# Elementwise work taken off GpSimd in a scheduled eight-core decoder trunk, with new planning costs and six square tiles

## The chip, the cores and the metric

The kernel runs on the 8 cores of one Trainium2 chip, one sequence of the batch per core, with no communication between the cores. The metric is the time of one execution in device microseconds (us) on the slowest core. An execution can fall into a slow state: the cores of one die (cores 0 to 3, or 4 to 7), or of both, are granted a lower TensorE clock than in the other executions, and the time is longer. I compare fast executions with fast ones, and I read core 4.

## The reference, cut to what matters

```python
D_MODEL = 1024; BATCH = 8; SEQ = 2048; DEPTH = 2; D_FF = 2816

def modulate(x, g, mod):                       # every sub-layer begins with this
    shift, scale, gate = jnp.split(mod, 3, axis=-1)
    h = rmsnorm(x, g) * (1.0 + scale[:, None, :]) + shift[:, None, :]
    return h, gate[:, None, :]

def swiglu(h, w_in, w_out):
    g, u = jnp.split(h @ w_in, 2, axis=-1)
    return (jax.nn.silu(g) * u) @ w_out

# layer 0: SwiGLU, gated mixer AB, SwiGLU;  layer 1: SwiGLU, pooling mixer, SwiGLU; final RMSNorm
mod = c_act @ w_mod[l] + b_mod[l]              # (B, 9*D), one row per output of the conditioning
x = x + 0.5 * gate * swiglu(h, w_ffn_in[l, 0], w_ffn_out[l, 0])
...
```

Everything is float32 in the reference. The kernel multiplies in float16.

## The kernel before

Each core keeps its whole residual stream `X` on chip and goes through ten *phases*: four SwiGLUs and one AB mixer, each for two halves of 1024 tokens (`p` = 0, 1). The pooling mixer runs in the background of other phases. The SwiGLU input projection is a Strassen-like product with 7 instead of 8 block products. It needs sums of blocks of the weights (`piece_sums`) and of `H` (`h_sums`). Between two phases, at a *boundary*, the last down-projection of one phase adds into `X` and squares it for the next RMSNorm, while the `H` of the next phase is built for the other half of the tokens.

The program is not written in its final order. A list scheduler places each instruction at the earliest gap of its engine by *planned* costs and latencies, and each engine is given its list in that order. Where two engines are offered ("flex"), the one planned to end first is taken.

```python
class Sched:
    LAT = {"pe": 0.27, "act": 0.10, "dve": 0.10, "pool": 0.12, "sp": 0.05}
    ...
        choices = eng if isinstance(eng, list) else [(eng, fn, cost)]
        for e, f, c in choices:
            ...                                   # ready = latest of the dependences' ends + LAT
            t = self.tl[e].find(ready, c)
            if best is None or t + c < best[0] - 1e-9:
                best = (t + c, t, e, f, c)
    ...
    def c_act(n, src="ps"):
        return (0.20 if src == "ps" else 0.40) + n / 1200.0
    def c_dve(n, half=False):
        return 0.20 + n / (1920.0 if half else 960.0)
    def c_pool(n):
        return 0.20 + n * 1.9e-3
    def tt_(out, in0, in1, op, reads, writes, n=TT, half=False, flex=False):
        f = I("tensor_tensor", out=out, in0=in0, in1=in1, op=op)
        if flex:
            return add([("dve", f, c_dve(n, half)), ("pool", f, c_pool(n))], None, reads=reads, writes=writes)
        return add("dve", f, reads=reads, writes=writes, cost=c_dve(n, half))

    def piece_sums(pc):                           # block sums of a weight piece, float16
        tt_(v(4), v(2), v(3), ALU.add, [k(2), k(3)], [k(4)], half=True, flex=True)
        ...                                       # three more
    def square(c, t):                             # on ScalarE or GpSimd
        q = sq_rot.next()                         # one of NSQ = 4 tiles
        op = add([("act", I("activation", ..., func=AF.Square), c_act(TT, "sb")),
                  ("pool", I("tensor_tensor", ..., op=ALU.mult), c_pool(TT))], ...)
    tmp_rot = Rot((6, 7))                         # two normalisation tiles
    def apply_chunk(l, s, p, c, tt, place):       # H = X * rstd * scale + shift
        tm = tmp_rot.next()
        tt_(TP[:, tm, 0:TT], Xv(c, t), RS[:, t, :], ALU.mult, ..., flex=True)
        act(place.ap(c, tt), TP[:, tm, 0:TT], AF.Identity, ..., scale=AS[...], bias=MODT[...])

    # class Down, at the end of each of its 16 units of the last down-projection:
                stt(Xv(dch, t), PS[bk][:], GH[...], Xv(dch, t), ALU.mult, ALU.add, ...)   # residual
                if self.last:
                    self.flush_ones(NSQ - 1)      # TensorE sums earlier squares over partitions
                    self.sq.append((square(dch, t), t))
    ...
    def run_down(dn, rest):
        for n, (_, f) in enumerate(rest[:-1]):
            f()
            pump()                                # background work, and every 7th time a row product
```

A *row product* multiplies one row of `w_mod` with the conditioning vector on VectorE (`WMOD<-WMOD,CB` in the profile, in two halves of 512). There are 144 rows, 16 of them before the first phase can start.

## Time and profile before

| | before |
|---|---|
| executions before the prediction | 2138.98, 2265.44, 2384.79 us; one more, profiled, 2215.79 us (slow) |
| core 4 of the profile: span | 2127.6 us |
| TensorE (PE), VectorE (DVE), ScalarE (ACT), GpSimd (POOL) busy on core 4 | 1985, 1446, 901, 677 us |

The list of cores (core: span, mean granted clock) shows which cores to read. The first die was disturbed.

```profile
core 4: 2127.6 us, clock 0.967
...
die 0 (median of its cores): 2185.6 us, clock 0.947
die 1 (median of its cores): 2129.1 us, clock 0.969
```

From the page of core 4, part 1 (busy us, share, number of instructions) and the first line of part 4 (the chain of waits followed back from the end):

```profile
PE 1985.1 (93%) x9440; PEld 913.4 (43%) x9440; DVE 1446.4 (68%) x2530; ACT 900.6 (42%) x1462; POOL 676.7 (32%) x707
...
PE 85%; DVE 12%; ACT 1%; DMA 1%; issue 0%; SPq 0%; DVEq 0%
```

TensorE bounds the kernel, but 12% of the chain passes through VectorE. Where that is, the stretches show. Each line is a window in us from the start; after its length come busy us and instructions of each engine, the granted clock (1.00 is the highest in the record), and the DMA share. The first five are boundaries, the sixth is the middle of a phase.

```profile
270.00:299.00 29.00, 16.70 (x72) 6.67 (x71) 28.83 (x34) 14.38 (x21) 21.97 (x16) 0.85 0.32 75
705.00:740.00 35.00, 25.60 (x116) 11.00 (x115) 33.11 (x35) 19.39 (x29) 31.02 (x24) 0.92 0.36 61
925.00:965.00 40.00, 30.35 (x136) 12.97 (x135) 38.90 (x51) 20.14 (x30) 31.82 (x26) 0.93 0.43 103
1150.00:1195.00 45.00, 33.36 (x148) 14.07 (x147) 43.36 (x58) 20.18 (x31) 33.89 (x27) 0.92 0.43 95
1375.00:1417.00 42.00, 36.54 (x163) 15.80 (x162) 34.98 (x46) 23.47 (x36) 24.98 (x21) 0.96 0.30 51
...
1450.00:1550.00 100.00, 100.00 (x519) 48.43 (x518) 55.97 (x91) 43.33 (x70) 27.12 (x29) 1.00 0.45 78
```

TensorE is not idle in this stretch in the middle of a phase, and at the boundaries it idles for 5 to 12 us while VectorE is occupied for 83 to 99% of the time. The clock also falls below 1.00 there: behind most of these gaps the clock record of this trace stands at 0.50 for 7 to 14 us, from the steady start (the first matmul of the steady stream, at 64.6 us) to the last matmul. Ten matmuls at half clock took 4.47 us, and ten at full clock (1.00) 2.32 us. At one boundary two gaps, 1.44 and 2.67 us with three matmuls between them, went before it: the record has 0.50 from 1413.4 us, 1.0 us into the second gap, and the ten matmuls from 1415.84 us on took 4.47 us.

Are those VectorE microseconds work? The groups of VectorE's instructions, by shape (count | busy us, mean ns of one | idle before), answer that:

```profile
L318 DVE TENSOR_TENSOR ACTB<-TP,ps 128x512 f16<-128x512 f32 x368 | 250.9, 686 | 113.0 <-PE ps L318 81.8 <-ACT ps L318 27.9
L318 DVE SCALAR_TENSOR_TENSOR X<-ps,GH,X 128x512 f32<-128x512 f32 x320 | 235.1, 747 | 197.6 <-PE ps L318 197.2
L318 DVE TENSOR_TENSOR SLOTS<-SLOTS 128x512 f16<-128x512 f16 x478 | 227.8, 496 | 11.6 <-POOL SLOTS L318 5.2 <-DMA SLOTS<-win 1.1
L318 DVE SCALAR_TENSOR_TENSOR WMOD<-WMOD,CB 128x512 f32<-128x512 f32 x256 | 216.5, 874 | 0.0
...
L318 DVE TENSOR_TENSOR TP<-X,RS 128x512 f32<-128x512 f32 x89 | 100.1, 1136 | 7.3 <-ACT H L318 4.0 <-ACT WMOD L318 3.3
L318 DVE TENSOR_TENSOR H<-H 128x1024 f16<-128x1024 f16 x64 | 62.2, 991 | 2.2 <-ACT H L318 1.5
```

`TP<-X,RS` (normalisation) and `ACTB<-TP,ps` both take two inputs of 512 elements, but the one with two inputs in SBUF takes 1136 ns and the one with an input in PSUM 686. (`ps`, the tiles that matmuls write to, lies in PSUM; the other tiles named here lie in SBUF.) A piece of the timeline at a boundary (start us, us, engine, instruction, idle before) shows what happens:

```profile
1401.85 1.99 DVE L318 TENSOR_TENSOR H<-H 128x1024 f16<-128x1024 f16 x1
...
1401.99 2.98 POOL L318 TENSOR_TENSOR TP<-X,RS 128x512 f32<-128x512 f32 x2
```

One H sum lasts 1.99 us when a GpSimd normalisation runs beside it. Of the 64 H sums in this trace 39 last 0.68 or 0.69 us; 32 of them overlap no two-input instruction of GpSimd, 7 do. The other 25, of 0.85 to 2.16 us, all overlap one, by 0.41 us or more. The residual additions, with one input in PSUM, average 745 ns where they overlap one and 748 where they do not. So I take part of VectorE's busy time for waiting. I call this lengthening of instructions with two SBUF inputs beside GpSimd's the *exclusion* of the two engines.

### The profile page before, as it was taken

What the parts mean: (1) busy time and instruction counts of PE and PEld (TensorE: products, weight loads), DVE (VectorE), ACT (ScalarE), POOL (GpSimd) and SP (SyncE); (2) the same over time, 40 slices, a digit from 0 to 9 for tenths busy, and PEclk for the clock granted to TensorE, in tenths of its full rate; (3) what the DMA queues carried; (4) which work ended last, traced back from release to release, by engine and by line L of the source; (5) the groups of instructions that cost most, each with busy time, mean ns of one, the idle gap of its engine ahead of it and who ended that gap; (6) DMA issues with size and microseconds to landing.
All of it is one profiled execution on the core that took longest, in us unless ns stands there. A gap on an engine that the chain in (4) does not pass through costs nothing.

```text
span 2214.1 us, 26222 instructions; the slowest of 8 cores (2125.3 to 2214.1 us)
## 1 busy us (share of the span) xinstructions
PE 2069.2 (93%) x9440; PEld 933.4 (42%) x9440; DVE 1444.3 (65%) x2530; ACT 900.9 (41%) x1462; POOL 676.9 (31%) x707
## 2 busy tenths in 40 slices
PE   2799979999999899989999799999999999999996
PEld 0344434444545344434444344444454345534442
DVE  6856887476767866686557863466565756575654
ACT  3433444045252551444214440355455544554242
POOL 5313353123111621162213431142244323442310
PEclk9999988889999999998889888899999999999998
DMA  9795948577666468756858474454635463536752
GB/s 278 149 234 111 174 91 145 109 132 149 114 113 125 76 102 164 125 116 114 147 110 147 92 114 65 64 81 67 95 57 77 59 104 53 81 51 101 145 86 76
DMA packets 71245, 248.75 MB, mean 112 GB/s; under 512 B 6992, under 2 KB 7120, under 8 KB 70608
## 3 DMA queue, kind: packets, MB, share of 16 engines
q0 software_dynamic: 46928, 153.63, 48.1%
q1 hardware_dynamic: 24192, 93.45, 13.4%
q8 instruction: 79, 1.29, 0.2%
q14 instruction: 46, 0.38, 0.1%
HBM read 392.28 MB, written 8.39 MB: 181 GB/s over the span
## 4 chain that ended last, share of the span: by engine, by line
PE 84%; DVE 12%; DMA 2%; ACT 1%; issue 0%; SPq 0%; DVEq 0%
PE ps L318 84%; DVE TP L318 2%; DVE X L318 2%; DVE SLOTS L318 2%; DVE WMOD L318 2%; DMA WMOD<-wmod 2%; DVE H L318 2%; DVE ACTB L318 1%; DVE MODT L318 0%; ACT H L318 0%; ACT SQ L318 0%; ACT RS L318 0%; DVE ps L318 0%; ACT ps L318 0%; SPq L318 0%
## 5 line engine op out<-in xcount | busy, mean ns | idle before, releaser
L318 PE MATMUL ps<-H,SLOTS 128*128 128x512 f16 x5440 | 1271.7, 394 | 88.8 <-DVE H L318 27.1
L318 PEld LDWEIGHTS ps<-H,SLOTS 128*128 128x128 f16 x5440 | 544.3, 101 | 774.3 <-issue 299.2
L318 PE MATMUL ps<-ACTB,SLOTS 128*128 128x512 f16 x3072 | 734.5, 395 | 0.0
L318 ACT ACTIVATE ps<-ps 128x512 f32<-128x512 f32 x528 | 307.3, 582 | 702.7 <-PE ps L318 670.1
L318 PEld LDWEIGHTS ps<-ACTB,SLOTS 128*128 128x128 f16 x3072 | 310.2, 101 | 388.0 <-issue 108.7
L318 DVE SCALAR_TENSOR_TENSOR X<-ps,GH,X 128x512 f32<-128x512 f32 x320 | 235.1, 746 | 221.6 <-PE ps L318 221.2
L318 DVE TENSOR_TENSOR ACTB<-TP,ps 128x512 f16<-128x512 f32 x368 | 251.5, 687 | 142.1 <-PE ps L318 103.0
L318 POOL TENSOR_TENSOR SLOTS<-SLOTS 128x512 f16<-128x512 f16 x226 | 286.8, 1272 | 182.8 <-DVE SLOTS L318 166.5
L318 POOL DMA_DIRECT2D SLOTS<-win x176 | 99.5, 565 | 781.0 <-PE ps L318 749.8
L318 ACT ACTIVATE TP<-ps 128x512 f32<-128x512 f32 x400 | 238.8, 597 | 202.1 <-PE ps L318 202.0
L318 DVE TENSOR_TENSOR TP<-ps,TP 128x512 f32<-128x512 f32 x176 | 121.5, 691 | 268.8 <-ACT ps L318 268.1
L318 DVE SCALAR_TENSOR_TENSOR WMOD<-WMOD,CB 128x512 f32<-128x512 f32 (+1 forms) x262 | 225.5, 888 | 16.5 <-DMA WMOD<-wmod 16.5
L318 DVE TENSOR_TENSOR SLOTS<-SLOTS 128x512 f16<-128x512 f16 x478 | 227.4, 495 | 11.7 <-POOL SLOTS L318 5.1
L318 ACT ACTIVATE SQ<-X 128x512 bf16<-128x512 f32 x165 | 103.2, 630 | 254.3 <-DVE X L318 200.8
L318 POOL TENSOR_TENSOR TP<-X,RS 128x512 f32<-128x512 f32 x103 | 148.0, 1443 | 64.5 <-ACT H L318 58.5
L318 DVE TENSOR_TENSOR ps<-ps,TP 128x512 f32<-128x512 f32 x176 | 122.9, 698 | 45.9 <-PE ps L318 45.7
L318 ACT ACTIVATE H<-TP,MODT,AS 128x512 f16<-128x512 f32 x160 | 125.8, 803 | 49.2 <-DVE TP L318 24.7
L318 POOL DMA_DIRECT2D SLOTS<-wout x64 | 47.1, 735 | 239.5 <-PE ps L318 232.4
L318 PE MATMUL ps<-SQ,ONES 128*128 128x512 bf16 x232 | 86.0, 407 | 29.9 <-ACT SQ L318 25.4
L318 DVE TENSOR_TENSOR TP<-X,RS 128x512 f32<-128x512 f32 x89 | 98.0, 1113 | 7.1 <-ACT H L318 4.0
L318 POOL TENSOR_TENSOR SQ<-X 128x512 bf16<-128x512 f32 x59 | 63.0, 1080 | 38.4 <-DVE X L318 18.2
L318 DVE TENSOR_TENSOR H<-H 128x1024 f16<-128x1024 f16 x64 | 62.2, 990 | 2.2 <-ACT H L318 1.5
(68 smaller groups left out, 515.1 us busy)
## 6 DMA issues: line engine op xcount, KB each, us to landing
SLOTS<-win POOLq DMA_DIRECT2D x176, 512.0 KB, 6.0
WMOD<-wmod SPq DMA_DIRECT2D x134, 512.0 KB, 6.2
SLOTS<-wout POOLq DMA_DIRECT2D x32, 768.0 KB, 9.5
SLOTS<-wout POOLq DMA_DIRECT2D x32, 640.0 KB, 8.2
SLOTS<-wab POOLq DMA_DIRECT2D x28, 512.0 KB, 7.4
X<-xT SPq DMA_DIRECT2D x4, 2048.0 KB, 17.4
outT<-X SPq DMA_DIRECT2D x16, 512.0 KB, 5.3
ACTB<-wmod SPq DMA_DIRECT2D x10, 512.0 KB, 21.1
```

The costliest lines, as they stand in the source:

```text
L318: return lambda E: getattr(E, name)(*a, **k)
```

## The change

Its intent is to leave GpSimd with loads and a few tiny instructions, to plan with costs nearer to the measured ones, and to relieve VectorE at the boundaries. The core of the diff:

```diff
-    LAT = {"pe": 0.27, "act": 0.10, "dve": 0.10, "pool": 0.12, "sp": 0.05}
+    LAT = {"pe": 0.27, "act": 0.16, "dve": 0.14, "pool": 0.12, "sp": 0.05}
-    NSQ = 4
+    NSQ = 6
-        return (0.20 if src == "ps" else 0.40) + n / 1200.0
+        return (0.10 if src == "ps" else 0.18) + n / 1200.0
-        return 0.20 + n / (1920.0 if half else 960.0)
+        return 0.09 + n / (1920.0 if half else 960.0)
...    # tt_ loses flex: block sums and normalisations always on VectorE
-        op = add([("act", I("activation", out=SQ[:, q, :], in_=Xv(c, t), func=AF.Square), c_act(TT, "sb")),
-                  ("pool", I("tensor_tensor", out=SQ[:, q, :], in0=Xv(c, t), in1=Xv(c, t), op=ALU.mult), c_pool(TT))],
-                 None, reads=[Xk(c, t)], writes=[("SQ", q)])
+        op = act(SQ[:, q, :], Xv(c, t), AF.Square, [Xk(c, t)], [("SQ", q)], src="sb")
...    # pump(rows=...) : row products are left out where rows is False
     def run_down(dn, rest):
         for n, (_, f) in enumerate(rest[:-1]):
             f()
-            pump()
+            pump(rows=not dn.last)
...    # pm_consts (bands of the pooling mixer): uses RS instead of TP tiles, called after the first loads
```

More of the change, by code (lines that the diff above doesn't have):

```diff
@@ L391, in act, with tt_ @@
         return add("act", I("activation", out=out, in_=in_, func=func, **kw), reads=reads, writes=writes, cost=c_act(n, src))
-    def tt_(out, in0, in1, op, reads, writes, n=TT, half=False, flex=False):
-        f = I("tensor_tensor", out=out, in0=in0, in1=in1, op=op)
-        if flex:
-            return add([("dve", f, c_dve(n, half)), ("pool", f, c_pool(n))], None, reads=reads, writes=writes)
-        return add("dve", f, reads=reads, writes=writes, cost=c_dve(n, half))
+    def tt_(out, in0, in1, op, reads, writes, n=TT, half=False):
+        return add("dve", I("tensor_tensor", out=out, in0=in0, in1=in1, op=op), reads=reads, writes=writes, cost=c_dve(n, half))
     def stt(out, in0, scalar, in1, op0, op1, reads, writes, n=TT, **kw):
@@ L514, in k @@
             return ("SL", s, q)
-        tt_(v(4), v(2), v(3), ALU.add, [k(2), k(3)], [k(4)], half=True, flex=True)
-        tt_(v(2), v(0), v(2), ALU.subtract, [k(0), k(2)], [k(2)], half=True, flex=True)
-        tt_(v(5), v(4), v(0), ALU.subtract, [k(4), k(0)], [k(5)], half=True, flex=True)
-        tt_(v(6), v(1), v(5), ALU.subtract, [k(1), k(5)], [k(6)], half=True, flex=True)
+        tt_(v(4), v(2), v(3), ALU.add, [k(2), k(3)], [k(4)], half=True)
+        tt_(v(2), v(0), v(2), ALU.subtract, [k(0), k(2)], [k(2)], half=True)
+        tt_(v(5), v(4), v(0), ALU.subtract, [k(4), k(0)], [k(5)], half=True)
+        tt_(v(6), v(1), v(5), ALU.subtract, [k(1), k(5)], [k(6)], half=True)
     wm_rot = Rot(range(NWM))
@@ L633, in bg_step, with pump @@
             bg_state[0] = 0.0
-    def pump(n=1):
+    def pump(n=1, rows=True):
         for _ in range(n):
@@ L638, in pump @@
                 bg_step()
-        rows_pump()
+        if rows:
+            rows_pump()
     def bg_drain():
@@ L728, in apply_chunk @@
         tm = tmp_rot.next()
-        tt_(TP[:, tm, 0:TT], Xv(c, t), RS[:, t, :], ALU.mult, [Xk(c, t), ("RS", t)], [("TP", tm)], flex=True)
+        tt_(TP[:, tm, 0:TT], Xv(c, t), RS[:, t, :], ALU.mult, [Xk(c, t), ("RS", t)], [("TP", tm)])
         act(place.ap(c, tt), TP[:, tm, 0:TT], AF.Identity, [("TP", tm)] + fin["k", l, s, c], [place.key(c, tt)], src="sb",
@@ L944, in ab_phase @@
             ab_consts()
-        bsb = [SQ, None]
-        def proj(lhs_slot, col, c, tt, b, first, last, cols=slice(0, TT), rhs=None):
-            pass
         def v_stats(tt, n):
@@ L1070, in pm_consts @@
             add("dve", I("memset", INVC[:, k:k + 1], 1.0 / (k + 1)), writes=[("INVC", k)], cost=0.1)
-        onesf = TP[:, 0, 0:128]
-        eye = TP[:, 1, 0:128]
-        rot = Rot(range(2, 8))
-        add("dve", I("memset", onesf, 1.0), writes=[("TP", 0)], cost=0.2)
-        add("pool", I("affine_select", out=eye, in_=onesf, pattern=[[1, 128]], compare_op=ALU.is_equal, fill=0.0,
-                      base=0, channel_multiplier=-1), reads=[("TP", 0)], writes=[("TP", 1)], cost=0.6)
+        onesf = RS[:, 2, 0:128]
@@ L1077, in pm_consts, with sel @@
+        eye = RS[:, 2, 128:256]
+        B1 = RS[:, 2, 256:384]
+        V = RS[:, 2, 384:400]
+        K = ("RS", 2)
+        add("dve", I("memset", onesf, 1.0), writes=[K], cost=0.2)
+        def sel(out, in_, pattern, op, base, cm):
+            add("pool", I("affine_select", out=out, in_=in_, pattern=[[pattern, 128]], compare_op=op, fill=0.0, base=base,
+                          channel_multiplier=cm), reads=[K], writes=[K], cost=0.6)
+        sel(eye, onesf, 1, ALU.is_equal, 0, -1)
         for i in range(4):
@@ L1078, in pm_consts @@
             w = 2 ** (i + 1)
-            b1 = rot.next()
-            B1 = TP[:, b1, 0:128]
-            add("pool", I("affine_select", out=B1, in_=onesf, pattern=[[1, 128]], compare_op=ALU.is_ge, fill=0.0,
-                          base=0, channel_multiplier=-1), reads=[("TP", 0)], writes=[("TP", b1)], cost=0.6)
-            add("pool", I("affine_select", out=B1, in_=B1, pattern=[[-1, 128]], compare_op=ALU.is_ge, fill=0.0,
-                          base=w - 1, channel_multiplier=1), reads=[("TP", b1)], writes=[("TP", b1)], cost=0.6)
@@ L1085, in pm_consts @@
-            stt(BANDv[i], eye, -float(w), B1, ALU.mult, ALU.add, [("TP", 1), ("TP", b1)], [("BAND", i)], n=128)
-            add("pool", I("affine_select", out=BPREVv[i], in_=onesf, pattern=[[-1, 128]], compare_op=ALU.is_ge, fill=0.0,
-                          base=-(129 - w), channel_multiplier=1), reads=[("TP", 0)], writes=[("BPREV", i)], cost=0.6)
-            v = rot.next()
-            V = TP[:, v, 0:16]
-            add("dve", I("memset", V, 0.0), writes=[("TP", v)], cost=0.1)
+            sel(B1, onesf, 1, ALU.is_ge, 0, -1)
@@ L1091, in pm_consts @@
+            sel(B1, B1, -1, ALU.is_ge, w - 1, 1)
+            stt(BANDv[i], eye, -float(w), B1, ALU.mult, ALU.add, [K], [("BAND", i), K], n=128)
+            sel(B1, onesf, -1, ALU.is_ge, -(129 - w), 1)
+            add("dve", I("tensor_copy", BPREVv[i], B1), reads=[K], writes=[("BPREV", i), K], cost=0.2)
+            add("dve", I("memset", V, 0.0), reads=[K], writes=[K], cost=0.1)
             for t in range(w - 1):
-                add("dve", I("memset", TP[:, v, t:t + 1], float(w - 1 - t)), reads=[("TP", v)], writes=[("TPc", v, t)], cost=0.1)
@@ L1093, in pm_consts @@
-            tt_(V, V, TP[:, 1, 0:16], ALU.mult, [("TP", v), ("TP", 1)] + [("TPc", v, t) for t in range(w - 1)], [("TP", v)], n=16)
-            tt_(BAND0v[i][:, 0:16], V, BANDv[i][:, 0:16], ALU.add, [("TP", v), ("BAND", i)], [("BAND0", i)], n=16)
+                add("dve", I("memset", V[:, t:t + 1], float(w - 1 - t)), reads=[K], writes=[("V", t)], cost=0.1)
+            tt_(V, V, eye[:, 0:16], ALU.mult, [K] + [("V", t) for t in range(w - 1)], [K], n=16)
+            tt_(BAND0v[i][:, 0:16], V, BANDv[i][:, 0:16], ALU.add, [K, ("BAND", i)], [("BAND0", i), K], n=16)
@@ L1115, in pm_gen @@
                     sh = l * 72 + s * 24
-                    tt_(TP[:, tm, 0:TT], Xv(ch, t), RS[:, t, :], ALU.mult, [Xk(ch, t), ("RS", t)], [("TP", tm)], flex=True)
+                    tt_(TP[:, tm, 0:TT], Xv(ch, t), RS[:, t, :], ALU.mult, [Xk(ch, t), ("RS", t)], [("TP", tm)])
                     op = act(PMH[:, 2 * c + tt, :], TP[:, tm, 0:TT], AF.Identity, [("TP", tm), "PMFREE"] + fin["k", l, s, ch],
@@ L1185, in build_nc @@
     rstd([0, 1], True)
-    pm_consts()
     for n, q in enumerate(rows0):
@@ L1205, in build_nc @@
         load_next(s, [gates[s]])
+    pm_consts()
     for lm in range(2):
```

## The prediction

> **What bounds the kernel now.** TensorE. The profile is of the slow state (list of cores: clock 0.947 on die 0, 0.969 on die 1); I read core 4, 2128 us, of the undisturbed die. On its page PE is busy 93%; PE is 85% and VectorE 12% of the chain of waits. A warm 128x512 matmul takes 0.216 us (ten in 2.16 us in the timeline), so all 9440 need about 1946 us (estimate). The other 180 us: 64 of start, 16 of tail, 100 at nine phase boundaries. Mid-phase PE is busy 100.0%.
>
> At the boundaries VectorE is full (28.8 of 29 us, 33 of 35, 39 of 40, 43 of 45; later 35 of 42), and PE idles 12.3, 9.4, 9.7, 11.6, later 5.5 us each. After most of them the clock is halved for 7 to 14 us[...], matmuls after the gaps are 0.43 us apart. Boundaries thus lose about 60 us idle plus 30 us of half clock.
>
> **What the change does.** GpSimd loses 226 block sums (1.27 us each), 103 normalisations (1.44) and 59 squares (1.08): 498 of its 677 us.
> - VectorE gains 226 x 0.42 + 103 x 0.68 = 165 us.
> - But VectorE and GpSimd exclude each other[...]: VectorE's normalisations average 1.14 us against 0.68 undisturbed, row products 0.87 against 0.69, H sums 0.99 against 0.66, block sums 0.50 against 0.42, small adds 0.58 against 0.16. That excess, 40+47+21+36+10 = 155 us, should vanish; VectorE stays near 1455 us (1445 to 1490).
> - ScalarE gains 59 x 0.63 = 37 us, 42% to 44%.
> - Row products leave the last down-projection; six square tiles let squares lag.
> - The new scheduling costs match measured durations better, so the static order should fit.
>
> **On the critical path.** Boundaries: a 38 us down-projection needs of VectorE about 16 x 0.67 + 16 x 0.64 + 8 x 0.67 + 15 x 0.40 + a few = 33 to 36 us undisturbed: it just fits. I expect 25 us idle instead of 60 and 15 us of half clock instead of 30: some 45 us saved, less 5 for new small waits mid-phase. Start: 11 more normalisations (7 us)[...], statistics 1 us later: 0 to 4 us saved. The pool constants stay hidden behind the first loads.
>
> **Prediction.** In the fast state about 2090 us against 2139 (2.3% less; range 2060 to 2125). Only one of the three runs before was fast (2139, 2265, 2385)[...], so the median may be slow: 2098 us, 2060 to 2260. In fast runs: faster by over 2% 0.55, within 2% 0.42, slower 0.03.
>
> **Right or wrong.** Right: VectorE normalisations at 0.7, row products 0.7, H sums 0.67 us; GpSimd under 180 us; VectorE 1.44 to 1.49 ms; gaps at later boundaries under 3 us, first steady matmul still at 60 to 66 us. Wrong: VectorE over 1550 us, or PE below 99% mid-phase.
>
> **What would make it wrong.** VectorE's strict order delaying an addition that PE waits for, as costs now have no margin; row products bunched at a boundary; ScalarE's 0.80 us outputs, planned shorter, holding the two normalisation tiles; or the excess being another wait.

The sum for the start came to 0 to 4 us saved: 7 us of normalisations and 1 us of later statistics against a saving of about 11 us. An estimate of the figure alone, from the trace before: up to the steady start the row products of 1024 elements and the one-column additions to `MODT` together last 11.5 us longer than if each took the shortest time of its kind there (1.21 and 0.15 us). The 0.66 us of an undisturbed H sum was a little low: the shortest in that trace takes 0.675.

## More of the kernel before

Last, what TensorE waited for over the whole run (total us, times, longest):

```profile
PE ps L318 <- DVE H L318: 27.4, 7, 5.2
PE ps L318 <- ACT H L318: 26.5, 12, 4.4
PE ps L318 <- ACT SQ L318: 25.4, 19, 8.4
...
```

The lines left out are short, but for two waits of 21.1 and 14.7 us in the first 65 us, before the steady stream of matmuls.

## The result, and the profile after

| | before | after |
|---|---|---|
| executions, us | 2265.44, 2138.98, 2384.79, 2138.36 | 2053.12, 2052.96, 2053.21, 2054.29 |
| median, us | 2202.21 | 2053.16 |
| fast runs, after over before | | 0.9601 (95%: 0.9578 to 0.9624) |
| core 4: TensorE idle after the steady start | 73.8 us | 15.5 us |
| core 4: time at half clock after it | 75.7 us | 9.6 us |
| core 4: steady start | 64.6 us | 66.8 us |

Ratios here are the mean time of one kernel's fast runs over that of the other's of the same rounds, so not quite the ratio of the medians. The idle time and the half-clock time were summed from the trace (gaps between matmul records, and the clock record) from the first matmul of the steady stream to the last matmul. In the profile after, 36 of 9440 matmul records are missing, which makes its idle time uncertain by some 2 us; the control below, with all records, shows 14.9. The two overlap, so they are indicators and do not add up to the difference.

From the page of core 4 after:

```profile
PE 1959.7 (96%) x9404; PEld 910.8 (44%) x9440; DVE 1437.7 (70%) x2863; ACT 935.6 (46%) x1521; POOL 173.8 (8%) x319
...
PE 93%; DVE 3%; DMA 2%; ACT 1%; issue 0%; SPq 0%; DVEq 0%
```

VectorE has 333 instructions more and is busy 9 us *less*. Its share of the chain of waits went from 12% to 3%. The groups that answer to those of before:

```profile
L318 DVE TENSOR_TENSOR SLOTS<-SLOTS 128x512 f16<-128x512 f16 x704 | 283.5, 420 | 12.4 <-DMA SLOTS<-win 3.7
L318 DVE TENSOR_TENSOR ACTB<-TP,ps 128x512 f16<-128x512 f32 x368 | 252.0, 687 | 110.0 <-PE ps L318 74.8 <-ACT ps L318 31.6
L318 DVE SCALAR_TENSOR_TENSOR X<-ps,GH,X 128x512 f32<-128x512 f32 x320 | 236.0, 749 | 160.0 <-PE ps L318 154.6
L318 DVE SCALAR_TENSOR_TENSOR WMOD<-WMOD,CB 128x512 f32<-128x512 f32 x256 | 167.6, 683 | 3.7 <-DMA WMOD<-wmod 3.6
L318 DVE TENSOR_TENSOR TP<-X,RS 128x512 f32<-128x512 f32 x192 | 127.3, 688 | 6.4 <-ACT H L318 2.9 <-ACT WMOD L318 2.1 <-ACT RS L318 1.3
L318 DVE TENSOR_TENSOR H<-H 128x1024 f16<-128x1024 f16 x64 | 42.6, 685 | 3.1 <-ACT H L318 2.7
```

The groups with an input in PSUM are where they were (687 and 749 ns); every group above with two inputs in SBUF fell to its undisturbed time (420, 683, 688 and 685 ns). The boundaries of before, and the same mid-phase stretch:

```profile
264.00:293.00 29.00, 26.71 (x123) 11.91 (x123) 26.15 (x50) 21.75 (x32) 1.59 (x3) 1.00 0.39 73
681.00:716.00 35.00, 29.71 (x130) 12.90 (x130) 30.18 (x50) 23.07 (x36) 1.58 (x3) 0.95 0.52 92
894.00:934.00 40.00, 39.22 (x181) 17.70 (x182) 36.13 (x68) 27.53 (x42) 2.13 (x4) 1.00 0.40 66
1102.00:1147.00 45.00, 44.22 (x204) 19.96 (x205) 37.61 (x69) 31.92 (x48) 2.65 (x5) 1.00 0.49 93
1316.00:1358.00 42.00, 41.22 (x190) 18.63 (x192) 35.92 (x64) 29.23 (x43) 2.66 (x5) 1.00 0.34 56
...
1450.00:1550.00 100.00, 98.85 (x574) 50.90 (x574) 63.40 (x119) 59.33 (x101) 6.53 (x11) 1.00 0.40 69
```

TensorE now idles 0.8 us at three of the boundaries, 2.3 at the first, and 5.3 at the one behind the AB mixer, the only one of the five where the clock still dips. Mid-phase it lost up to 1.15 us in 100; before, one of eight mid-phase stretches lost 1.02. What TensorE waited for:

```profile
...
PE ps L318 <- ACT SQ L318: 10.7, 3, 7.3
PE ps L318 <- DVE H L318: 6.7, 7, 2.2
PE ps L318 <- ACT H L318: 5.6, 2, 3.8
...
```

(The two start waits are 23.2 and 15.9 us now, and 9.3 of the 10.7 us for squares are in the start as well.) The waits for `H` fell from 54 us to 12.

Where the 79.1 us of core 4 came from, by phase (from the first matmul fed by `H` of one phase to that of the next; F is a SwiGLU with layer and number, AB the mixer, the digit behind the dash the half of the tokens):

| us | F00-0 | F00-1 | AB-0 | AB-1 | F01-0 | F01-1 | F10-0 | F10-1 | F11-0 | F11-1 and end |
|---|---|---|---|---|---|---|---|---|---|---|
| before | 247.0 | 226.8 | 105.3 | 109.6 | 226.2 | 230.3 | 224.1 | 239.2 | 238.5 | 240.6 |
| after | 239.4 | 215.6 | 102.3 | 106.0 | 219.0 | 213.2 | 213.1 | 231.7 | 230.8 | 235.6 |

A SwiGLU phase without background work holds 984 matmuls of 512 columns, which at 0.216 us (an estimate, from ten in 2.16 us between starts in the timeline) is 212.5 us. Two phases after are within 1 us of that. The start of the steady stream came 2.2 us *later* in this profile.

### The profile page after: what moved, and what is told of

The parts are those of the page before. It is cut to its first block, busy times and chain, and to the rows that moved or that the text cites. A ratio compares the mean times of both kernels' runs of the same rounds, so it can differ in the third digit from the quotient of the medians.

```text
span 2051.6 us, 26107 instructions; the slowest of 8 cores (2048.1 to 2051.6 us)
## 1 busy us (share of the span) xinstructions
PE 1964.0 (96%) x9440; PEld 910.6 (44%) x9440; DVE 1438.8 (70%) x2863; ACT 935.7 (46%) x1521; POOL 173.7 (8%) x319
## 4 chain that ended last, share of the span: by engine, by line
PE 92%; DVE 3%; DMA 3%; ACT 1%; issue 0%; SPq 0%; DVEq 0%
PE ps L318 92%; DMA ACTB<-wmod 1%; DVE X L318 1%; DMA X<-xT 1%; DMA WMOD<-wmod 1%; DVE TP L318 1%; DVE WMOD L318 0%; DVE ACTB L318 0%; ACT SQ L318 0%; DVE H L318 0%; ACT H L318 0%; DVE ps L318 0%; ACT RS L318 0%; ACT L318 0%; ACT ps L318 0%
## 5 line engine op out<-in xcount | busy, mean ns | idle before, releaser
L318 PE MATMUL ps<-H,SLOTS 128*128 128x512 f16 x5440 | 1208.9, 380 | 50.8 <-DVE SLOTS L318 23.1
L318 PEld LDWEIGHTS ps<-H,SLOTS 128*128 128x128 f16 x5440 | 530.4, 98 | 688.1 <-issue 65.2
L318 PE MATMUL ps<-ACTB,SLOTS 128*128 128x512 f16 x3072 | 693.7, 380 | 0.0
L318 DVE TENSOR_TENSOR ACTB<-TP,ps 128x512 f16<-128x512 f32 x368 | 252.3, 688 | 109.6 <-PE ps L318 74.5
L318 DVE TENSOR_TENSOR SLOTS<-SLOTS 128x512 f16<-128x512 f16 x704 | 284.1, 420 | 16.3 <-DMA SLOTS<-win 7.5
L318 ACT ACTIVATE SQ<-X 128x512 bf16<-128x512 f32 x224 | 137.7, 627 | 184.1 <-DVE X L318 135.8
L318 DVE SCALAR_TENSOR_TENSOR WMOD<-WMOD,CB 128x512 f32<-128x512 f32 (+1 forms) x262 | 175.2, 697 | 11.7 <-DMA WMOD<-wmod 11.6
L318 DVE TENSOR_TENSOR TP<-X,RS 128x512 f32<-128x512 f32 x192 | 127.5, 689 | 5.7 <-ACT H L318 2.9
L318 PE MATMUL ps<-SQ,ONES 128*128 128x512 bf16 x232 | 83.8, 402 | 15.6 <-ACT SQ L318 10.8
L318 PEld LDWEIGHTS ps<-SQ,ONES 128*128 128x128 bf16 x232 | 23.0, 99 | 49.5 <-issue 25.6
L318 DVE TENSOR_TENSOR H<-H 128x1024 f16<-128x1024 f16 x64 | 42.7, 686 | 3.1 <-ACT H L318 2.7
L318 ACT ACTIVATE WMOD<-TP,MODT,AS 128x512 f16<-128x512 f32 x32 | 25.2, 806 | 16.1 <-DVE TP L318 15.7
```

The lines of the kernel that those rows point to most:

```text
L318: return lambda E: getattr(E, name)(*a, **k)
```

## The experiments

Three explanations were to be told apart. **L**: the exclusion of VectorE and GpSimd had prolonged VectorE's work, and its end is the gain. **O**: the better static order, from truer planned costs, is the gain. **G**: results of GpSimd itself came late in the chain, as one normalisation takes it 1.44 us against 0.69. All outputs are right. The first call met a chip on which *every* kernel was throttled, the kernel before too (2316.91 to 2427.42 us; the cores' mean clocks in all runs there were 0.80 to 0.95); its times carry little, its traces still do (matmul records are missing from them too, which again leaves their idle times uncertain by some 2 us). The other two calls ran on one chip with fast runs of the kernel before at 2132.78 to 2137.08 us.

Measured on that second chip, with idle and half-clock time of core 4 after the steady start. The three ratios between 0.98 and 0.99 are differences of under 2%, but clear of the noise: their 95% intervals are 0.9817 to 0.9856, 0.9824 to 0.9871 and 0.9880 to 0.9919, in the order of the table.

| run | median of all runs, us | ratio to before, fast runs | idle, us | half clock, us |
|---|---|---|---|---|
| before (first profile) | 2135.5 | 1 | 73.8 | 75.7 |
| only the engine move | 2099.51 | 0.9837 | 44.3 | 47.8 |
| only the costs | 2102.60 | 0.9847 | 54.4 | 29.8 |
| the change | 2051.36 | 0.9613 | 14.9 | 10.2 |
| the change, rows back | 2057.26 | 0.9641 | 17.8 | 17.9 |
| the change, four squares | 2040.32 | 0.9560 | 6.1 | 4.8 |
| the change and 160 useless additions | 2113.85 | 0.9899 | 62.3 | 23.7 |
| the change, four squares, third tile | 2035.01 | 0.9531 | 3.9 | 0.0 |
| the same with a higher ScalarE cost | 2039.79 | 0.9553 | 8.5 | 5.6 |

### Useless GpSimd additions (e4_idle_adds, then e4b_idle_adds)

```diff
+    DUM = sb("DUM", [128, 512], F32)
...    # after everything else is placed; resid: the 160 residual additions of last down-projections
+    for o in resid:
+        d = add("pool", I("tensor_tensor", out=DUM[:], in0=DUM[:], in1=DUM[:], op=ALU.add), writes=["DUM"], cost=1.4, after=o.end + 0.14)
+        d.deps = d.deps | {o.idx}
```

The order on TensorE, VectorE and ScalarE was compared and is that of the changed kernel; nobody waits for `DUM`. Only GpSimd's activity differs.

> The changed kernel, with the same order on VectorE, TensorE and ScalarE, plus one useless GpSimd addition of 128x512 float32 (two reads) behind each of the 160 residual additions of the phases' last down-projections; nobody waits for them. Theory L: VectorE's two-input SBUF groups grow (normalisations from 0.69 to about 1.0, H sums from 0.69 to about 0.9 us), PSUM-fed groups do not, and TensorE idles at the boundaries again: 2070 to 2110 us. Rivals O (order) and G (the latency of GpSimd results in the chain): 2050 to 2060 us, as nothing waits for the additions.

On the throttled chip it took 2283.55 to 2294.87 us apart from one run at 2363.69, with TensorE idle 54.3 us on core 4. It was repeated:

> The changed kernel with 160 useless GpSimd additions, again, in the hope of an unthrottled chip. In the throttled run TensorE idled 54 us instead of 15 and half clock rose from 10 to 24 to 34 us, so I expect 2051 plus 39 plus about 10: 2085 to 2110 us. Without an exclusion 2050 to 2058 us.

Measured: 2113.85 us, 62 us more than the changed kernel (2051.36 us, same chip). It was run at another time. The size was missed by a little upwards; the direction and the groups are as theory L says. GpSimd's group, and VectorE's:

```profile
L318 POOL TENSOR_TENSOR DUM<-DUM 128x512 f32<-128x512 f32 x160 | 201.4, 1259 | 145.7 <-DVE X L318 139.2 <-PE ps L318 2.2
```

```profile
L318 DVE TENSOR_TENSOR ACTB<-TP,ps 128x512 f16<-128x512 f32 x368 | 252.2, 687 | 110.7 <-PE ps L318 75.6 <-ACT ps L318 31.3
...
L318 DVE TENSOR_TENSOR TP<-X,RS 128x512 f32<-128x512 f32 x192 | 182.1, 976 | 3.7 <-ACT WMOD L318 2.1 <-ACT RS L318 1.1 <-ACT H L318 0.5
...
L318 DVE TENSOR_TENSOR H<-H 128x1024 f16<-128x1024 f16 x64 | 57.6, 919 | 2.3 <-ACT H L318 1.4
```

201 us of GpSimd additions, 1.26 us each, made VectorE's busy time grow from 1437.1 (control) to 1531.3 us. The normalisation went from 688 to 976 ns and the H sum from 685 to 919; the PSUM-fed group did not move. So the exclusion is shown, and also that it alone, without any result of GpSimd in the chain, cost 62 us here, where it falls on the boundaries. A rival is that the additions delay the weight loads, which GpSimd issues; but TensorE waited for a load once in this run, 15.6 us in the start, and 14.9 in the control. What TensorE waited for in this run:

```profile
PE ps L318 <- ACT SQ L318: 38.9, 56, 6.4
...
PE ps L318 <- DVE H L318: 17.0, 7, 2.8
```

The new wait is for ScalarE's squares, 56 times. I read it so: the residual additions leave VectorE late, so their squares are late, and the small matmul that sums a square stands in TensorE's list in front of the next unit. The trace before has such a place: TensorE idled 1.14 us for a square, summed it at 1406.72 us, and began the ten matmuls of the next unit at 1406.93.

Theory G is not tested alone by any run, as the engine move ends both the exclusion and the late results. But the trace before leaves it little room. GpSimd does not appear in its chain of waits, and these are the waits for a GpSimd result by ScalarE's `H` and by TensorE in the whole run (total us, times, longest):

```profile
ACT H L318 <- POOL TP L318: 1.8, 3, 1.3
...
PE ps L318 <- POOL SQ L318: 0.5, 1, 0.5
```

### Useless GpSimd memsets (e5_idle_memsets)

```diff
-        d = add("pool", I("tensor_tensor", out=DUM[:], in0=DUM[:], in1=DUM[:], op=ALU.add), ...)
+        d = add("pool", I("memset", DUM[:], 0.0), writes=["DUM"], cost=0.7, after=o.end + 0.14)
+        add("pool", I("memset", DUM[:], 0.0), writes=["DUM"], cost=0.7, after=d.end)
```

> As the run with the useless additions, but each is replaced by two GpSimd memsets, which read nothing. If the exclusion is of GpSimd instructions that read SBUF: within 0.3% of the changed kernel, 2048 to 2060 us, no VectorE group longer. If any GpSimd activity or its semaphores slow VectorE: as slow as the useless additions in proportion to GpSimd's busy time.

This ran on the throttled chip, so the expected microseconds could not be met: 2249.69 us, where the additions took 2293.65 and the kernel before 2326.22 (medians of all runs, most of them slow). Where both dies ran alike the three took 2252.73, 2283.55 and 2326.22 us, one run each. The groups decide it:

```profile
L318 POOL MEMSET DUM<- 128x512 f32 x321 | 169.6, 528 | 141.0 <-DVE X L318 128.6 <-POOLq L324 0.4
```

```profile
L318 DVE TENSOR_TENSOR TP<-X,RS 128x512 f32<-128x512 f32 x192 | 126.7, 685 | 6.7 <-ACT H L318 2.9 <-ACT WMOD L318 2.3 <-ACT RS L318 1.4
L318 DVE TENSOR_TENSOR H<-H 128x1024 f16<-128x1024 f16 x64 | 42.7, 686 | 3.1 <-ACT H L318 2.7
```

In the same call the additions had brought these groups to 980 and 919 ns. 170 us of GpSimd memsets prolong no group with two SBUF inputs, and TensorE idles 16.2 us, about as in the changed kernel. (One group of 16 instructions with one large input, `ACTB<-TP,STAT`, went from 546 to 575 ns, 0.5 us in all.) So for the instructions with two SBUF inputs here it is GpSimd's reading of SBUF that excludes, not its activity: the additions, which read it, prolonged them, and the memsets, which only write it, left them at 685 and 686 ns. The two large groups with one input in PSUM took 686 to 688 and 746 to 749 ns before, after, and in both these runs.

### Only the engine move (e9_only_engines)

```diff
 # the kernel before, with the old costs, rows, four squares and constants
-    def tt_(out, in0, in1, op, reads, writes, n=TT, half=False, flex=False):
+    def tt_(out, in0, in1, op, reads, writes, n=TT, half=False):       # always VectorE
...    # square: ScalarE alone, as in the change
```

> The kernel before with only the engine move: block sums and normalisations on VectorE, squares on ScalarE; old costs, rows, squares and constants. From the first call (old costs in the changed kernel: TensorE idle 46 us, half clock 63 us, although no VectorE group was prolonged) I expect idle 45 to 60 us, half clock 55 to 75 us: about 20 us off the time before and 40 to 60 us above the control. Theory L alone (end of the exclusion is the gain) expects within 1% of the control.

Measured: 2099.51 us, 36 us below the kernel before and 48 above the control. VectorE's groups were free (H sum 686 ns, normalisation 689), but TensorE idled 44.3 us.

```profile
L318 DVE TENSOR_TENSOR TP<-X,RS 128x512 f32<-128x512 f32 x192 | 129.1, 689 | 5.7 <-ACT H L318 2.7 <-ACT WMOD L318 2.0
```

The gain was larger than the 20 us that I had read off the throttled run; the 48 us to the control is in the expected span, and idle and half clock (47.8 us) came out a little below it. What TensorE waited for:

```profile
PE ps L318 <- ACT H L318: 27.1, 12, 4.0
...
PE ps L318 <- DVE H L318: 8.3, 7, 1.4
```

The wait for VectorE's H sums fell from 27.4 to 8.3 us, but that for ScalarE's `H` stayed at 27. So the undisturbed VectorE alone does not fill the boundaries: theory L alone falls.

### Only the costs (e2_only_costs, then e2b_only_costs), and the old costs in the changed kernel (e1_old_costs)

```diff
 # e2, e2b: the kernel before with LAT, c_act and c_dve of the change
 # e1: the changed kernel with LAT, c_act and c_dve of before
```

> The kernel before with only the new cost and latency constants; GpSimd still takes 258 elementwise instructions (388 before). Theory L: VectorE's groups stay prolonged (normalisations near 1.0 us) and the time stays at 2095 to 2140 us. Rival O: most of the gain comes, 2055 to 2085 us.

> The changed kernel with the scheduler's old cost and latency constants, all else as changed. Theory L (the gain is the end of the VectorE-GpSimd exclusion, the order hardly matters): within 1% of the changed kernel, 2050 to 2073 us, VectorE busy near 1440 us. Rival O (the gain is the better static order): most of the gain is lost, 2090 to 2130 us, with idle of 5 us and more at the phase boundaries although no VectorE group is slower.

Both first ran on the throttled chip, so their times (2281.81 and 2324.8 us) tell nothing. The traces do. With the old costs in the changed kernel VectorE's groups are all at their short times, yet TensorE idles 46.1 us on core 4, and its waits for ScalarE's `H` add up to 35.6 us: the same picture as in the run with only the engine move. With only the new costs the normalisation stays at 1.08 us. Of the two, only the run with the costs alone was repeated:

> The kernel before with only the new cost and latency constants, again, in the hope of an unthrottled chip. The engine move alone gave 2099.5 us against 2135.5. If costs and engine move add up, costs alone give about 2135 minus 50, 2080 to 2090 us. If the costs need the undisturbed VectorE to be true, they give less alone: 2095 to 2125 us, with TensorE idle of about 50 us (52 in the throttled run).

Measured: 2102.60 us, in the second of the two spans, with TensorE idle 54.4 us. The new order was planned for a VectorE that GpSimd does not disturb; where it does (the normalisation takes 1079 ns here, the H sum 1059), as I read it, the squares come late:

```profile
PE ps L318 <- ACT SQ L318: 52.0, 35, 7.4
```

So theory O alone falls too. Costs alone gave 33 us, the engine move alone 36, and the changed kernel with four squares, which has both, the rows rule and the new place of the constants, 95. With the 6 us of the rows below, 75 are accounted for by single parts. Some 20 us come from having both at once (or from the constants, which were not run alone). The constants can hardly be it: in the trace after they are done 15.2 us after the start, and VectorE then idles 7.2 us until the first row has landed. Nor is such a sum exact: two square tiles fewer moved the time by 11 us and one planned cost by 5 us (below), so the split into parts may be off by that much.

### Row products back at the boundary (e6_rows_back), and the control (c1_changed)

```diff
-            pump(rows=not dn.last)
+            pump()
```

> The changed kernel again, as the control of this call, as the chip of the first call was throttled for all kernels. Both theories: TensorE idle about 15 us after the start, half clock about 10 us; 2053 us on an untroubled chip.

> The changed kernel with row products issued between the units of the last down-projections again. If keeping them out mattered (VectorE is full there): TensorE idle 20 to 30 us instead of 15, and 5 to 15 us longer than the control. If it did not: within 0.2% of the control.

The control took 2051.36 us, 15 us idle. With the rows back it took 2057.26 us: 6 us for that part, within what was expected, though idle rose only to 17.8 us; the half-clock time rose from 10.2 to 17.9.

### Four square tiles (e7_four_squares)

```diff
-    NSQ = 6
+    NSQ = 4
```

> The changed kernel with four square tiles instead of six. If the lag matters: TensorE waits for squares at the boundaries again, 3 to 15 us longer than the control. If it does not: within 0.2% of it.

A miss in sign: 2040.32 us, 11 us *faster* than six. The extra tiles were no gain; they shift the static order. In the control the last seven outputs to `H` behind the AB mixer pile up on ScalarE after the last residual, and TensorE waits for them:

```profile
707.88 5.53 ACT L318 ACTIVATE H<-TP,MODT,AS 128x512 f16<-128x512 f32 x7
...
711.12 1.44 PE L318 MATMUL ps<-H,SLOTS 128*128 128x512 f16 x3 [3.80 <-ACT H L318]
```

With four tiles three outputs are left at that place, and the stretches of the two boundaries show it (the first and second of before):

```profile
264.00:293.00 29.00, 28.38 (x133) 12.72 (x131) 26.99 (x51) 21.01 (x32) 1.58 (x3) 1.00 0.38 69
676.00:711.00 35.00, 32.56 (x151) 14.16 (x149) 32.67 (x59) 26.78 (x41) 2.11 (x4) 1.00 0.60 116
```

Why the scheduler packs better with four was not taken apart further: tile counts enter its gap search at many places.

### A third normalisation tile (e11_third_tile), and a higher ScalarE cost (e12_third_tile_act_cost)

The memory of the two freed square tiles goes to one more normalisation tile.

```diff
-    NTP = 8
+    NTP = 9
-    NSQ = 6
+    NSQ = 4
-    tmp_rot = Rot((6, 7))
+    tmp_rot = Rot((6, 7, 8))
 # e12 besides: a ScalarE instruction from SBUF is planned at
-        return (0.10 if src == "ps" else 0.18) + n / 1200.0
+        return (0.10 if src == "ps" else 0.28) + n / 1200.0
```

> The changed kernel with four square tiles, and the freed memory used for a third normalisation tile. At the boundaries VectorE then waits less for ScalarE to free one of two tiles (0.2 to 0.3 us each in the trace): 2032 to 2041 us if those waits still hold TensorE up, no change from the 2040 us of four squares if not.

> As the run with the third tile, and the planned cost of a ScalarE instruction from SBUF set to 0.71 us for 512 elements, the spacing that the trace shows for the H outputs, instead of 0.61. If the order still suffers from that under-estimate: 1 to 8 us below the run with the third tile. If not: within 0.2% of it.

The third tile gave 2035.01 us, the fastest kernel: 16 us below the change and 100 below the kernel before. It came later on the same chip as the four squares; the runs of each lie within 2 us, so the 5 us between them are clear. TensorE idles 3.9 us after the start and is never at half clock.

The higher ScalarE cost is a miss: 2039.79 us, 5 us *slower*, although 0.71 us is the spacing that the trace shows. A truer single cost need not give a better order, as the search is greedy.

## Why the prediction was right or wrong

The range (2060 to 2260 us around 2098) was for the median and did not hold 2053; the narrower fast range (2060 to 2125) did not either. The forecast "faster by over 2%" came true, at 4.0% in fast runs against the 2.3% named.

- **What bounds the kernel: right.** TensorE mid-phase before was 99 to 100% busy, and the gain is at the boundaries, as the phase table shows.
- **The exclusion: right in kind and size.** I put the excess at 155 us and VectorE's gained work at 165. Busy time went from 1446 to 1438 us, so about 175 vanished (1446 + 165 − 1438 = 173). The useless additions and memsets show what it hangs on: normalisations took 976 ns beside additions that read SBUF, and 685 beside memsets. Row products at 0.68, H sums at 0.69, normalisations at 0.69 and GpSimd at 174 us are as foretold. VectorE fell 7 us short (1438) of the lower end of 1445 to 1490.
- **The mis-sized term: the boundaries.** The step that failed reads "I expect 25 us idle instead of 60 and 15 us of half clock instead of 30: some 45 us saved". Measured: idle 73.8 to 15.5 us after the steady start, and half-clock time, half of which is loss (ten matmuls 4.47 us instead of 2.32), 75.7 to 9.6. The ten phases together shrank by 81 us where I had 45. My sum said that VectorE's 33 to 36 us "just fit" into a 38 us down-projection, and I then took off for an imperfect order. The runs show that the order lost less than that: with true costs *and* an undisturbed VectorE two phases came within 1 us of the matmuls alone, while each part without the other left 44 to 54 us idle. I had counted the two as one saving instead of asking what each leaves without the other. How much of the miss lies before and how much after can be estimated: from the steady start to the last matmul took 2046 us before and 1964 after, and the matmuls alone some 1945 (the third-tile run, never at half clock there, less its idle time). So 101 us were lost before, where I had 60 + 30, and 19 after, where I had 25 + 15 and 5 mid-phase. The larger part of the miss, 26 of 37 us, is the loss left after the change; 11 were in the trace before and I had not counted them.
- **New small waits mid-phase: right in kind, small in size.** Mid-phase windows after showed 98.1 to 100% busy, but the lowest (78.46 of 80 us) lacks matmul records: the control has 80.00 there, and 98.95 to 100% in all. My sign of being wrong, "PE below 99% mid-phase", was thus met in one window of eight and meant nothing for the time; a window before had 98.98% as well.
- **The start: wrong in sign.** I foretold 0 to 4 us saved; it came 2.2 us later in the first profile (64.6 to 66.8 us, just outside my sign of 60 to 66), though starts of other runs with the same start code, 64.7 to 66.8, show that this is within its scatter.
- **Rows and squares: half right.** Rows out of the boundary were worth 6 us. That "six square tiles let squares lag" was meant as a gain; with four the kernel was 11 us faster.
- **The slow state: not borne out, not settled.** I feared a slow median. In the result 4 of 4 runs after were fast; on the second chip of the experiments, 8 runs of the control and of the third tile were, as against 10 of 14 of the kernel before, but 1 of 4 was slow in four of the variants. The cores' mean clocks were 0.979 to 0.995 in all 8 executions of the change that are in the result and the control, with TensorE busy 96% of the profiled one of the result; in the first profile, a slow one, the clock record of core 0 stands at 0.81 for 477 us. Whether the change alters the odds is open.

## What to carry to other kernels

Before you count a busy engine as working, compare the mean duration of its instructions by where their inputs lie: here two-SBUF-input instructions of VectorE took up to 65% longer, on average, than their undisturbed time (normalisations 1136 against 688 ns) in the kernel before, whose GpSimd read SBUF beside them, and offloading half a millisecond of work to GpSimd had bought VectorE nothing. A static order rests on the durations it was planned with, so remove the contention and re-fit the costs together; each alone gave about two fifths of the gain here. But measure every new order: a truer ScalarE cost made it 5 us slower. Then test every buffer count of such a scheduler for itself: two extra square tiles cost 11 us, and the same memory as a normalisation tile brought 5.
